# The recurrence's opening: key products stored a second time in the inverses' layout, the first v load on GpSimd, one mask earlier

## The chip, the cores and the metric

The kernel runs on one core of a Trainium2 chip. Five engines work from queues of their own, each in order: TensorE (PE, with its weight loads as PEld), VectorE (DVE), ScalarE (ACT), GpSimd (POOL) and SyncE (SP). Transfers are given out by SP, ACT or GpSimd and carried out by 16 shared DMA engines. The metric is the time on the device in microseconds (us), lower is better.

## The reference

A two-layer hybrid over 256 tokens of width 2048, in float32. Layer 0 is an RWKV7 mixer with 32 heads of 64: four projections `r, k, v, z`, a decay and a gate from low-rank products, and the recurrence. Layer 1 is an attention with three branches (compressed, selected, window), which plays no part here.

```python
mixed = u[None] + xx[None] * mu[:, None, None, :]
rkvz = jnp.einsum('nbtd,nde->nbte', mixed[:4], w_rkvz)
...
def step(S, inp):                       # the recurrence, once per token
    r_t, w_t, k_t, v_t, a_t, b_t = inp
    sa = jnp.einsum('bhvk,bhk->bhv', S, a_t)
    S = S * w_t[:, :, None, :] + sa[..., None] * b_t[:, :, None, :] + v_t[..., None] * k_t[:, :, None, :]
    return S, jnp.einsum('bhvk,bhk->bhv', S, r_t)
```

## The kernel before

**Weights.** Weight matrices stream through PE in pieces. SP loads a piece of 512 KB (`wraw`, L178, five buffers), ACT copies each half into a rounded high part (`whi`, L206), DVE subtracts to get the low part (`wlo`, L191), and PE multiplies three times (high by high, low by high, high by low: L569, L570, L572, or L587, L588, L589 where the weight is the stationary side). These matmuls are the bulk of the kernel. In the recurrence they serve as filling between its small steps: `fill(n)` runs some of them from the projection of `r`.

**The recurrence by chunks.** The 256 tokens are four chunks of 64, and the 32 heads are 16 pairs `j`. Within a chunk, the token-by-token recurrence is turned into matrix products with the inverse of a triangular 64x64 matrix. In the *key phase* (up to about 348 us) `stage_k(j)` forms that matrix's key products `ab` for the pair `j` (L726), copies them to `abs` (L728) and stores 128x256 of them to the scratch tensor `abd` in HBM (L729). `stage_t(b)` inverts the 32x32 diagonal blocks of eight pairs at a time (`b` is 0 or 1), 128 blocks, one in each partition of `invA`; each block row is 32 numbers, 128 bytes. It reads these blocks from `abd` with eight transfers of 16x32x32 (L756); for `b` = 1 two of the eight go to GpSimd, the rest to SP. Then come many small DVE steps (L786 to L806), which the planner places one at a time ("pump"); the results go to `tnd` and `yvd` in HBM.

**The opening.** Two pairs make a unit U, and the recurrence runs through eight units. Unit 0 needs a prologue, and its order on every engine is that of the code (a manual schedule): load `spl` (the pair's scaled keys), `Yb`, `a`; clear `uv`; some filling; then the second inverse begins, and its input is loaded; load `t`; filling; load `Yb` of unit 1; filling; load `spl` of unit 1; and then `load_v(0)` on ACT's queue (four transfers of 64 KB from `vd` into `uv`, L932). After that the list `PROLOGUE` is worked off: `R` scales r (L960 to L963); a number is filling; `G` is a product whose result ACT copies to `gs` (L972, L974); `Y` multiplies by `gs` (L981) and completes the inverse in `Yb`; `B` transposes (L991); `V6` or `V9` are six or nine pumps of the second inverse on DVE; `A` forms attention products (L1005, L1007), `M2` masks one of them into AMA, `M0` and `M1` the other into AMR (L1013). Then the units' phases begin with the *removal* (L1022), which needs AMA and `uv`. After `Y`, `load_a(1)` gives GpSimd the `a` and `t` loads of unit 1.

## Time and profile before

| | |
|---|---|
| three runs | 1164.82, 1166.99, 1160.91 us; median 1164.82 |
| profiled execution | 1160.9 us; its span is 1160.9 us too, so next to nothing lies around it |
| instructions | 25551 |
| DMA packets | 231325, of them 49808 under 512 B |
| bytes moved | 225.26 MB, mean 194 GB/s |

Times are from the span's start. A timeline row has the start, the length, the engine, line and operation, out<-in by the program's names, the number of instructions put together, and in brackets the idle time ahead with what ended it. SPq, ACTq and POOLq are issues of transfers by these engines. In the table of waits stand the engine and line that waited, what for, the sum, the times and the longest. The columns of the stretches are told where one is shown.

### The profile page before, as it was taken

How to read it: one execution, taken by the hardware profiler on the slowest of the kernel's cores; microseconds unless marked ns; L12 is line 12 of the kernel's file. 1: busy time of each engine (PE TensorE's matmuls, PEld its weight loads, DVE VectorE, ACT ScalarE, POOL GpSimd, SP SyncE). 2: the span in 40 equal slices, each digit the busy share in tenths (PEclk: the TensorE clock that was granted, in tenths of full speed). 3: DMA queues.
4: the chain of work that ended last, by engine and by line, in shares of the span. 5: the costliest groups of instructions: out<-in, count | busy, mean ns of one | idle time of the engine just before them, and what ended most of it. 6: DMA issues, size and time to landing. Idle time of an engine off the chain costs nothing.

```text
span 1160.9 us, 25551 instructions
## 1 busy us (share of the span) xinstructions
PE 1121.0 (97%) x9414; PEld 981.0 (85%) x9414; DVE 843.0 (73%) x1876; ACT 715.4 (62%) x1680; POOL 328.1 (28%) x418
## 2 busy tenths in 40 slices
PE   7999999999997999998999999999999999999996
PEld 6878899888987888897788888887989989988886
DVE  6999966679895887566567876764577888785564
ACT  4767777577763456565556766665656666665453
POOL 1300045324346455563000010100333333333011
PEclk8999999999998999999999999999999999999999
DMA  6458877787869768874467758685745353635752
GB/s 230 157 186 245 237 211 247 234 201 209 258 213 245 196 176 254 234 201 128 125 209 247 209 174 275 186 259 161 195 136 152 96 148 106 164 95 185 282 186 105
DMA packets 231325, 225.26 MB, mean 194 GB/s; under 512 B 49808, under 2 KB 179200, under 8 KB 230816
## 3 DMA queue, kind: packets, MB, share of 16 engines
q1 hardware_dynamic: 225280, 218.55, 64.1%
q0 software_dynamic: 4832, 4.82, 1.8%
q8 instruction: 74, 1.21, 0.4%
q14 instruction: 51, 0.42, 0.1%
q10 hardware_dynamic: 1088, 0.26, 0.1%
HBM read 200.48 MB, written 23.10 MB: 193 GB/s over the span
## 4 chain that ended last, share of the span: by engine, by line
PE 81%; DVE 9%; DMA 3%; ACT 3%; issue 3%; SPq 1%; POOL 0%; ACTq 0%; POOLq 0%; DVEq 0%
PE bank L570 13%; PE bank L572 13%; PE bank L569 13%; PE bank L587 8%; PE bank L588 7%; PE bank L589 7%; PE bank L234 5%; DVE wlo L191 3%; PE pair L572 1%; PE pair L569 1%; ACT whi L206 1%; PE pair L570 1%; PE pair L1051 1%; PE bank L726 1%; DMA wraw<-in_b_w_o_dram 1%
## 5 line engine op out<-in xcount | busy, mean ns | idle before, releaser
L191 DVE TENSOR_TENSOR wlo<-wraw,whi 128x512 fp32r<-128x512 f32 (+2 forms) x616 | 437.8, 724 | 157.2 <-ACT whi L206 152.5
L206 ACT ACTIVATE whi<-wraw 128x512 fp32r<-128x512 f32 (+2 forms) x664 | 401.7, 620 | 209.4 <-PE bank L572 92.8
L587 PE MATMUL bank<-mh,whi 128*128 128x256 f32 (+1 forms) x800 | 236.1, 295 | 0.2 <-issue 0.2
L570 PE MATMUL bank<-wlo,mh 128*128 128x512 f32 (+3 forms) x608 | 229.1, 379 | 2.0 <-DVE wlo L191 2.0
L588 PE MATMUL bank<-ml,whi 128*128 128x256 f32 (+1 forms) x800 | 228.3, 285 | 1.1 <-issue 1.1
L589 PE MATMUL bank<-mh,wlo 128*128 128x256 f32 (+1 forms) x800 | 227.8, 285 | 0.0
L572 PE MATMUL bank<-whi,ml 128*128 128x512 f32 (+3 forms) x608 | 227.6, 377 | 0.0
L569 PE MATMUL bank<-whi,mh 128*128 128x512 f32 (+3 forms) x608 | 202.2, 378 | 0.8 <-ACT mh L419 0.8
L587 PEld LDWEIGHTS bank<-mh,whi 128*128 128x128 f32 (+1 forms) x800 | 151.8, 190 | 6.5 <-issue 0.9
L588 PEld LDWEIGHTS bank<-ml,whi 128*128 128x128 f32 (+1 forms) x800 | 152.3, 190 | 3.0 <-issue 1.3
L589 PEld LDWEIGHTS bank<-mh,wlo 128*128 128x128 f32 (+1 forms) x800 | 151.9, 190 | 1.3
L570 PEld LDWEIGHTS bank<-wlo,mh 128*128 128x128 f32 x608 | 114.3, 188 | 20.5 <-DVE wlo L191 3.1
L569 PEld LDWEIGHTS bank<-whi,mh 128*128 128x128 f32 x608 | 113.4, 188 | 19.0 <-ACT mh L419 1.1
L572 PEld LDWEIGHTS bank<-whi,ml 128*128 128x128 f32 x608 | 114.3, 188 | 17.8 <-issue 0.4
L191 POOL TENSOR_TENSOR wlo<-wraw,whi 128x512 fp32r<-128x512 f32 (+2 forms) x48 | 62.5, 1303 | 190.3 <-ACT whi L206 158.5
L570 PE MATMUL bank<-wlo,kvh 128*128 128x512 f32 x192 | 76.9, 401 | 0.0
L572 PE MATMUL bank<-whi,kvl 128*128 128x512 f32 x192 | 76.1, 396 | 0.0
L569 PE MATMUL bank<-whi,kvh 128*128 128x512 f32 x192 | 67.4, 396 | 0.0
L419 ACT ACTIVATE mh<-mtmp 128x256 fp32r<-128x256 f32 x96 | 38.9, 410 | 21.5 <-DVE mtmp L426 20.3
L426 DVE SCALAR_TENSOR_TENSOR mtmp<-xx,prm,xn 128x256 f32<-128x256 f32 x96 | 47.9, 506 | 1.2 <-POOL xx L458 1.0
L570 PEld LDWEIGHTS bank<-wlo,kvh 128*128 128x128 f32 x192 | 36.1, 188 | 8.7 <-issue 0.4
L420 DVE TENSOR_TENSOR ml<-mtmp,mh 128x256 fp32r<-128x256 f32 x96 | 41.6, 441 | 2.0 <-ACT mh L419 1.8
(332 smaller groups left out, 1871.3 us busy)
## 6 DMA issues: line engine op xcount, KB each, us to landing
wraw<-in_a_w_rkvz_dram SPq DMA_DIRECT2D x128, 512.0 KB, 5.2
wraw<-in_kv_w_dram SPq DMA_DIRECT2D x48, 512.0 KB, 4.6
wraw<-in_b_w_in_dram SPq DMA_DIRECT2D x40, 512.0 KB, 4.2
wraw<-in_a_w_o_dram SPq DMA_DIRECT2D x32, 512.0 KB, 4.6
wraw<-in_b_w_o_dram SPq DMA_DIRECT2D x32, 512.0 KB, 4.6
spd<-sp SPq DMA_DIRECT2D x16, 642.0 KB, 4.7
spl<-spd SPq DMA_DIRECT2D x16, 642.0 KB, 6.8
wraw<-in_b_w_in_dram SPq DMA_DIRECT2D x24, 384.0 KB, 3.3
```

The costliest lines, as they stand in the source:

```text
L191: eng.tensor_tensor(lv, src, hv.bitcast(F32), op=OP.subtract)
L206: self.nc.scalar.activation(hv, src, AF.Copy)
L234: return fn(*args, **kw)
L419: S.activation(h, src, AF.Copy)
L420: V.tensor_tensor(l, src, h.bitcast(F32), op=OP.subtract)
L426: V.scalar_tensor_tensor(m, xx[:, k, :], mu[:, k:k + 1], xn[:, k, 1:], op0=OP.mult, op1=OP.add)
L569: PE.matmul(o, mh[:, ts], wh[:, 0, :], start=k == ends[0], stop=False)
L570: PE.matmul(o, mh[:, ts], wl[:, 0, :], start=False, stop=False)
L572: PE.matmul(o, ml[:, ts], wh[:, 0, :], start=False, stop=k == ends[1])
L587: PE.matmul(o, wh[:, s, :], mh, start=k == 0 and first, stop=False, **kw)
L588: PE.matmul(o, wh[:, s, :], ml, start=False, stop=False, **kw)
L589: PE.matmul(o, wl[:, s, :], mh, start=False, stop=k == NK - 1, **kw)
```

## The change

Each pair's key products are stored twice: besides `abd`, four new transfers on SP (32x4x32 each, one for each head and half) write the two kinds of diagonal blocks into `abdd[b]`, which has the layout of `invA`, 1024 numbers for each of the 128 partitions. `stage_t` reads them in one transfer of 128x1024 on SP instead of eight. `load_v(0)` goes to GpSimd and stands behind `load_a(0, "T")`. In `PROLOGUE`, `M2` stands ahead of the second `V9`.

```diff
-PROLOGUE = ("R0", "R1", 6, "G", "B0", 4, "I", "Y", "B1", 2, "V6", "A0", 2, "V9", "A1", "V9", "M2", "M0", "M1", 2)
+PROLOGUE = ("R0", "R1", 6, "G", "B0", 4, "I", "Y", "B1", 2, "V6", "A0", 2, "V9", "A1", "M2", "V9", "M0", "M1", 2)
...
+    abdd = [dram.tile([128, 1024], F32, name=f"abdd{i}") for i in range(2)]
...
         nc.sync.dma_start(abd[j], abs_)
+        for h in range(2):
+            for q in range(2):
+                r0 = 64 * h + 32 * q
+                dst = bass.AP(tensor=abdd[j // 8].tensor, offset=abdd[j // 8].offset + (q * 16 + (j % 8) * 2 + h) * 1024,
+                              ap=[[32, 32], [32 * 1024, NCH], [1, 32]])
+                nc.sync.dma_start(dst, abs_[r0:r0 + 32, :].rearrange("p (c s) -> p c s", c=NCH)[:, :, 32 * q:32 * q + 32])
...
-        for c in range(NCH):
-            for q in range(2):
-                u0 = (c * 2 + q) * 16
-                src = bass.AP(tensor=abd.tensor, offset=abd.offset + 8 * b * 128 * T + q * 32 * T + c * 64 + q * 32,
-                              ap=[[64 * T, 16], [T, 32], [1, 32]])
-                (G if b and c == 3 else nc.sync).dma_start(A[u0:u0 + 16], src)
+        nc.sync.dma_start(A.rearrange("p a b -> p (a b)"), abdd[b])
...
     load_a(0, "T")
+    load_v(0, G)
     fill(10)
...
     fill(8)
-    load_v(0, nc.scalar)
```

PE's order does not change. In the rows below, brackets hold the semaphores that an instruction waits for: an engine's name, or a lane (DMAHW0 to 7 of SP and ACT, DMASW0 to 7 of GpSimd), on which the transfer that had the lane before must have landed.

SP at the end of the key phase and in the opening, before:

```order
L729 DMA abd<-abs 128x256 [waits Activation_49]
L923 DMA spl_4524<-spd 128x1284 [waits DMAHW2_49,PE_49]
...
L178 DMA wraw<-in_a_w_rkvz_dram 128x8x128 [waits DMAHW0_49,DVE_49]
L756 DMA invA<-abd 16x32x32 [waits DMAHW1_49]
L756 DMA invA<-abd 16x32x32 [waits DMAHW2_49]
L756 DMA invA<-abd 16x32x32 [waits DMAHW3_49]
L756 DMA invA<-abd 16x32x32 [waits DMAHW4_49]
L756 DMA invA<-abd 16x32x32 [waits DMAHW5_49]
L756 DMA invA<-abd 16x32x32 [waits DMAHW6_49]
L178 DMA wraw<-in_a_w_rkvz_dram 128x8x128 [waits DMAHW7_49,DVE_49]
```

and after:

```order
L730 DMA abd<-abs 128x256 [waits DMAHW6_49,Activation_49]
L736 DMA abdd_1612<-abs 32x4x32 [waits DMAHW7_49]
L736 DMA abdd_1612<-abs 32x4x32 [waits DMAHW0_49]
L736 DMA abdd_1612<-abs 32x4x32 [waits DMAHW1_49]
L736 DMA abdd_1612<-abs 32x4x32 [waits DMAHW2_49]
L925 DMA spl_4583<-spd 128x1284 [waits DMAHW3_49,PE_49]
...
L178 DMA wraw<-in_a_w_rkvz_dram 128x8x128 [waits DMAHW1_49,DVE_49]
L758 DMA invA<-abdd_1612 128x1024 [waits DMAHW2_49]
L178 DMA wraw<-in_a_w_rkvz_dram 128x8x128 [waits DMAHW3_49,DVE_49]
```

Four stores stand behind `abd`, the weight load waits for the lane of the third of them, and one issue stands where six were. Between the rows shown are, in both, the second `spl` and four `Yb`.

ACT ahead of `gs`, before:

```order
L206 ACTIVATE whi<-wraw 128x512 [waits DMAHW0_49,DVE_49,PE_49]
L932 DMA uv_4672<-vd 64x4x64 [waits DMAHW3_49]
L932 DMA uv_4672<-vd 64x4x64 [waits DMAHW5_49]
L932 DMA uv_4672<-vd 64x4x64 [waits DMAHW6_49]
L932 DMA uv_4672<-vd 64x4x64 [waits DMAHW7_49]
L206 ACTIVATE whi<-wraw 128x512 [waits DVE_49,PE_49]
L206 ACTIVATE whi<-wraw 128x512 [waits DMAHW0_49,DVE_49,PE_49]
L974 ACTIVATE gs<-pair_4913 128x256 [waits PE_49]
```

and after:

```order
L206 ACTIVATE whi<-wraw 128x512 [waits DMAHW5_49,DVE_49,PE_49]
L206 ACTIVATE whi<-wraw 128x512 [waits DVE_49,PE_49]
L206 ACTIVATE whi<-wraw 128x512 [waits DMAHW1_49,DVE_49,PE_49]
L976 ACTIVATE gs<-pair_4965 128x256 [waits PE_49]
L994 ACTIVATE bkt_4741<-pair_4927 128x384 [waits PE_49]
```

The four `uv` loads are gone from between the splits. DVE around the mask AMA, after:

```order
L795 TENSOR_TENSOR invX<-invT,invM 128x64 [waits DVE_49]
L797 TENSOR_TENSOR invM_4796<-invM_4796,invX 128x64 [waits DVE_49]
L1015 TENSOR_TENSOR ama_4733<-bank_4727,cst 128x512 [waits PE_49]
L795 TENSOR_TENSOR invX<-invT,invM 128x64 [waits DVE_49]
L797 TENSOR_TENSOR invM_4796<-invM_4796,invX 128x64 [waits DVE_49]
L799 COPY invT<-invM_4796 128x4x4x4 [waits DVE_49]
L805 TENSOR_TENSOR invX<-invA,invM_4796 128x128 [waits Activation_49]
```

Before, eleven more steps of the inverse, the four rows below it and seven like them, stood ahead of that mask; AMR keeps its place behind them. GpSimd, from its clearing of `uv` to the `Yb` loads of unit 1, after:

```order
L929 MEMSET uv_4731 64x8x64 [waits Pool_49]
L854 DMA t_4587<-tnd_1613 32x4x32 [waits DMASW2_49]
...
L934 DMA uv_4731<-vd 64x4x64 [waits DMASW6_49]
L934 DMA uv_4731<-vd 64x4x64 [waits DMASW7_49]
L934 DMA uv_4731<-vd 64x4x64 [waits DMASW0_49]
L934 DMA uv_4731<-vd 64x4x64 [waits DMASW1_49]
L1170 MEMSET ones_4746 128x2 [waits DMAHW3_49,PE_49,Pool_49]
L1171 MEMSET Yb_4730 128x512
L862 DMA Yb_4730<-yvd_1615 32x4x32 [waits DMASW2_49,Pool_49]
```

Two `invA` pieces, which stood between the clearing and the four `t` loads, are gone, and four `uv` loads stand behind `t`.

## The prediction

> **What bounds the kernel now.** I read the page first: the busy times, then the chain that ended last.

> ```profile
> PE 1121.0 (97%) x9414; PEld 981.0 (85%) x9414; DVE 843.0 (73%) x1876; ACT 715.4 (62%) x1680; POOL 328.1 (28%) x418
> PE 81%; DVE 9%; DMA 3%; ACT 3%; issue 3%; SPq 1%; POOL 0%; ACTq 0%; POOLq 0%; DVEq 0%
> ```

> TensorE (PE) is busy 97% of the span and carries 81% of the chain. So a change pays only where PE stands idle or runs at a lower clock, about 40 us of the 1160.9, and what it adds elsewhere costs only if PE waits for it. The table of stretches says where that is around the change: the key phase ahead of the recurrence, and then the opening.

> ```profile
> 300.00:348.00 48.00, 47.80 (x337) 41.53 (x336) 42.05 (x77) 33.78 (x78) 23.28 (x26) 1.00 0.76 237
> 348.00:385.00 37.00, 27.86 (x371) 26.36 (x369) 22.37 (x65) 12.38 (x27) 23.22 (x44) 0.86 1.11 252
> ```

> The columns are the length, the busy time of PE, PEld, DVE, ACT and POOL, PE's granted clock, the DMA share and GB/s. The key phase keeps PE busy 47.80 of 48 us. The opening leaves it idle 9.1 of 37 us, at a mean clock of 0.86, while the DMA engines are full (1.11). Next the waits between 345 and 385 us (sum, times, longest):

> ```profile
> PE pair L981 <- ACT gs L974: 7.0, 1, 7.0
> PE pair L1022 <- issue: 2.1, 1, 2.1
> ```

> Two waits of PE make all of it: 7.0 us before Y (L981) and 2.1 us before the removal (L1022). PE's timeline gives their places:

> ```profile
> 364.39 0.28 PE L589 MATMUL bank<-mh,wlo 128*128 128x256 f32 x1
> 371.71 1.08 PE L981 MATMUL pair<-gs,t 64*64 64x32 f32 x32 [7.04 <-ACT gs L974]
> 382.33 0.54 PE L1022 MATMUL pair<-uv,ama 128*64 128x64 f32 x8 [2.10 <-issue]
> 389.57 0.71 PE L972 MATMUL pair<-Yb,a 64*64 64x32 f32 x32
> ```

> and cutting the stretch finer gives the price of the clock:

> ```profile
> 364.70:371.70 7.00, 0.00 (x0) 0.02 (x1) 0.85 (x2) 1.51 (x4) 5.56 (x11) 0.71 0.97 221
> 371.70:378.00 6.30, 6.29 (x95) 5.89 (x95) 5.41 (x23) 2.57 (x6) 4.51 (x8) 0.51 1.10 312
> 378.00:382.30 4.30, 2.23 (x56) 1.82 (x56) 3.55 (x15) 0.52 (x2) 2.26 (x4) 1.00 1.21 252
> ```

> During the 7-us wait the clock falls, and the 6.3 us behind it run at 0.51. At full clock that work is 6.3 x 0.51 = 3.2 us, so the long wait costs another 3.1 us. Behind the 2.10-us wait the clock stays 1.00. The opening thus loses 7.0 + 3.1 + 2.1 = 12.2 us.

> Who holds gs (L974)? It has nothing but ACT's queue in front of it:

> ```profile
> 357.04 0.63 ACT L206 ACTIVATE whi<-wraw 128x512 fp32r<-128x512 f32 x1 [0.81 <-PE bank L588]
> 366.50 3.60 ACTq L932 DMA_DIRECT2D uv<-vd  x4
> 370.19 1.15 ACT L206 ACTIVATE whi<-wraw 128x512 fp32r<-128x512 f32 x2 [12.52 <-DMA wraw<-in_a_w_rkvz_dram]
> 371.25 0.36 ACT L974 ACTIVATE gs<-pair 128x256 f32<-128x256 f32 x1
> ```

> The row at 370.19 names a weight transfer, but that one was issued at 355.36 (SP's timeline, next) and had 14 us. What stood in the way are the four loads of v, which ACT issues only at 366.50, each waiting for its turn behind earlier transfers of SP:

> ```profile
> 348.66 1.73 SPq L729 DMA_DIRECT2D abd<-abs  x1
> 352.25 1.93 SPq L860 DMA_DIRECT2D Yb<-yvd  x4
> 355.36 0.40 SPq L178 DMA_DIRECT2D wraw<-in_a_w_rkvz_dram  x1
> 356.18 8.22 SPq L756 DMA_DIRECT2D invA<-abd  x6
> 364.50 2.10 SPq L178 DMA_DIRECT2D wraw<-in_a_w_rkvz_dram  x2
> ```

> SP needs 8.22 us for the six input pieces of the second inverse. So the chain is: slow issues on SP, then the v loads on ACT, then two splits, then gs, then Y.

> **The change, part by part.** *The v loads leave ACT.* Their 3.60 us and the wait ahead of them vanish from ACT. gs then stands behind the two splits (1.15 us), the second of which needs the weight piece issued now at 355.36. SP has four more stores ahead of it.

> ```profile
> abd<-abs SPq DMA_DIRECT2D x16, 128.0 KB, 4.9
> vd<-vst SPq DMA_DIRECT2D x16, 128.0 KB, 3.8
> uv<-vd SPq DMA_DIRECT2D x28, 64.0 KB, 4.8
> uv<-vd ACTq DMA_DIRECT2D x4, 64.0 KB, 8.8
> invA<-abd SPq DMA_DIRECT2D x14, 64.0 KB, 4.3
> wraw<-in_a_w_rkvz_dram SPq DMA_DIRECT2D x128, 512.0 KB, 5.2
> ```

> (times, KB each, median us from issue to landing.) No store of 128-byte runs is in the trace. A store's issue is bounded by a Yb issue (1.93 / 4 = 0.48 us) and the slow abd issue (1.73 us). I take 0.55, next to the Yb row, since those four are the same 32x4x32 pattern in the other direction: 4 x 0.55 = 2.2 us, which puts the weight issue at 357.6. It also waits for one of these stores to land; issued at 351.5 and with the 4.9 us of abd that is 356.4, so no more. Landing is 357.6 + 5.2 = 362.8, the splits end at 364.2 (1.15 us and the handover), gs at 364.6, and Y starts at 365.0, when PE has just run dry (364.39 + 0.28). Bounds: 364.7, and 369.7 if each store takes 1.73 us (4 x 1.18 = 4.7 us later). The long wait shrinks from 7.04 us to about 0.3, and with it goes the half clock: 3.1 us.

> The trace kept the clock through 2.10 us idle and lost it in 7.04. [...]

> *One inverse input instead of eight.* The eight pieces, 128-byte runs, 4096 packets, become one transfer with 4-KB runs. SP gives it out near 358.2, one issue of 0.4 us in place of 8.22. The nearest landing is 5.2 us (wraw, as many bytes): 363.4. On the far side stands spl (642 KB), given out behind abd (from 350.4) and waited for until 360.12, 9.7 us: 367.9.

> ```profile
> 360.12 0.43 DVE L960 TENSOR_TENSOR spl<-bank,spl 128x256 f32<-128x256 f32 x1 [1.50 <-DMA spl<-spd]
> ```

> spl too goes out 2.2 us later, so this work of DVE and the low half of the split behind it, which PE takes up about 1.2 us before it runs dry, move from 360.8 to 363.0; that is just in time for Y at 365.0, and I book nothing.

> *M2 ahead of the second V9.* DVE's rows of before, where AMA is the tensor that the removal waits for:

> ```profile
> 370.85 1.29 DVE L191 TENSOR_TENSOR wlo<-wraw,whi 128x512 fp32r<-128x512 f32 x2 [9.38 <-ACT whi L206]
> 373.62 0.18 DVE L767 COPY invT<-invA 128x16 f32<-128x16 f32 x1 [0.22 <-DMA spl<-spd]
> 378.13 0.22 DVE L795 TENSOR_TENSOR invM<-invM,invX 128x64 f32<-128x64 f32 x1
> 381.55 0.68 DVE L1013 TENSOR_TENSOR ama<-bank,cst 128x512 f32<-128x512 f32 x1
> ```

> By the order after, AMA follows the step at 378.13, so it starts 4.7 us behind the inverse's first copy (373.62 to 378.35) instead of 7.9. That copy follows DVE's halves of the splits and two clears. It came 2.3 us behind the end of the splits on ACT (370.19 + 1.15 = 371.3, against 373.62); from their end at 364.2 I get 366.5, still behind the landing at 363.4. AMA runs from 371.2 to 371.9, and the removal starts at 372.0. PE's own work between Y and the removal is 3.2 + 2.2 = 5.4 us at full clock, so it is dry from 370.5 and waits 1.5 us. With 367.9 for the landing the removal is at 373.4. The gain of the opening is 382.33 - 372.0 = 10.3 us; the losses agree: 6.7 of the long wait, 3.1 of clock, 0.6 of the short one are 10.4.

> *What comes late next.* GpSimd's queue now carries the four v loads, and behind them are the eight Yb loads of unit 1, two scalings and the a and t loads of unit 1, which G and Y of unit 1 wait for.

> ```profile
> 356.71 1.26 POOL L756 DMA_DIRECT2D invA<-abd  x2 [4.03 <-issue]
> 357.96 2.19 POOL L852 DMA_DIRECT2D t<-tnd  x4
> 364.57 3.26 POOL L860 DMA_DIRECT2D Yb<-yvd  x6 [2.42 <-DMA invA<-abd]
> 369.73 0.57 POOL L849 DMA_DIRECT2D a<-abd  x1
> t<-tnd POOLq DMA_DIRECT2D x32, 16.0 KB, 4.6
> ```

> Two input pieces of the inverse leave this queue, with their 1.26 us and the 4.03 us that they waited for SP. So t goes out from 352.7 and v from 354.9, to 357.5 with 2.19 us and some room. The last Yb load waits for the last v load to land: 357.5 plus 4.8 (SP's row) to 8.8 (ACT's, in the crowded stretch), 362.3 to 366.3. I take 364. Then come one more issue (0.55) and the scalings with 1.9 (from 364.57 + 3.26 to 369.73 before), so a starts at 366.5; the eight issues need 8 x 0.57 = 4.6 us, and t's last lands near 366.5 + 4.6 + 4.6 = 375.7, at worst 378. G of unit 1 is due at 389.57 - 10.3 = 379.3, its Y 1.3 us later. It is covered by 1.3 to 3.8 us; if the cover is gone, what is over is lost one for one. I take 0.3 us.

> *Stores in the key phase.* 16 times four stores of 16 KB. PE stays busy if SP's weight loads are not late, and SP mostly waits for its consumers there (165 to 348 us):

> ```profile
> SPq L178 <- DVE wlo L191: 38.5, 20, 4.0
> ```

> Ahead of weight loads alone that is 38.5 us of free time of SP. 64 stores at 0.48 to 1.73 us are 31 to 111 us, at my 0.55 they are 35. The DMA engines: the crowded stretch at 362 to 366 us moved

> ```profile
> DMA packets 2268, 0.36 MB, mean 90 GB/s; under 512 B 2194, under 2 KB 2265, under 8 KB 2267
> ```

> in 4 us, 1.8 ns a packet with all sixteen engines full. 512 packets per head pair are 0.9 us, sixteen of them 14 us in 183, 8% more on a share of 0.76. I book 0.5 us, with 0 to 2 as bounds; it can't gain. The landing of the first inverse's input falls beside filled PE and counts nothing.

> Sum: 10.3 - 0.3 - 0.5 = 9.5 us. The profiled execution has 1160.9 us and is the fastest of the three runs; the median, 1164.8, is 3.9 above it. Against the profile I get 1151.4, against the median 1155.3; I say 1155.

> **The rivals.** *A, the wait only shortens.* If a store takes 1.73 us, or if it lands late and the weight piece behind it waits, Y starts at 369.7, a wait of 5.0 us. If this drops the clock, 5.4 us of work need 8.5 and the removal is at 378.2: gain 4.1, less 0.8, 3.3, hence 1161.5 against the median, within 0.5%. For it: the slow abd issue stands at this very place, and the engines are full. Against it: the Yb issues right behind it took 0.48. [...]

> *B, GpSimd's queue becomes the bound.* If v needs more than 8.8 us there, or a start waits for lanes, G of unit 1 waits 2 to 4 us: 1158. For it, v, Yb, a and t then stand in one queue; against it, 1.3 us of cover even at the ACT row's 8.8.

> *C, slower.* The stores hold up the weights throughout the key phase. At 1.73 us each they need 111 us of SP, far more than those 38.5 us; where a weight load comes 1 us late per head pair, 16 us are lost: 1171. Above 0.6 us per pair the gain is gone, above 1 us it is slower by 0.5%. Against it, only the last abd issue is slow in this trace.

> *D, it does not do what it says*: gs is held by the weight piece alone, as the row at 370.19 names it. Then Y stays at 371.7 and M2 alone gives 2.1 us: 1163. The 14 us since that piece's issue speak against it.

> **How the numbers follow.** The forecast 0.65, A 0.13, B 0.10, C 0.06, D 0.06. A measurement of this kernel tells some 0.5% (5.8 us) from no change. The forecast's own range is 1151 (10.3 and no give-back, on a run at the profile's level) to 1158. For 8 in 10, I add B and A and reach to 1162; the low end is 1149, if the short wait goes too. Faster by over 0.5% is below 1159: nearly all of the forecast, most of B and the milder third of A, 0.74; same, the rest of A and B, D, 0.20; slower, 0.06.

> **What would show it.** Y within 1.5 us after PE runs dry, and no clock under 1.00 behind it; the removal 7 us behind Y; one invA of 4-KB runs landing ahead of 367; no longer v rows on ACT; G of unit 1 without a wait; PE in 300 to 348 us still at 47.5 or more. The prediction is wrong if PE waits over 2 us at Y or at G of unit 1, or if waits for wraw turn up in the key phase.

## The result, and the profile after

The kernel after takes 1154.39 us (median of 4 runs, 1152.51 to 1156.80), the one before 1165.90 beside it: a ratio of 0.9914, interval 0.9895 to 0.9932. Timed a second time, beside two of the experiments, it took 1152.49 us, 0.9901 (0.9882 to 0.9921). 1155 had been forecast. The ratios and their 95% intervals are the ones on record; a gain in us below is worked out from the ratio, and the quotient of two medians differs from it by up to 0.0015 (1.7 us). The profiled execution has a span of 1153.6 us, 7.3 less than that of before; a second profile of the same kernel has 1150.4, 10.5 less.

The two stretches that were shown of before:

```profile
300.00:348.00 48.00, 47.88 (x340) 41.98 (x341) 42.23 (x78) 32.67 (x76) 24.84 (x29) 1.00 0.77 235
348.00:385.00 37.00, 32.17 (x529) 30.02 (x529) 27.23 (x82) 17.09 (x40) 24.29 (x45) 1.00 1.10 294
```

In the same 37 us PE is busy 32.2 us instead of 27.9, and now all of it at full clock: 1.00 instead of 0.86. The key phase, with its added stores, is as full as before. The waits of PE between 345 and 385 us:

```profile
PE pair L1024 <- issue: 2.0, 1, 2.0
PE bank L993 <- DVE mb L963: 1.6, 1, 1.6
PE pair L983 <- issue: 0.7, 1, 0.7
```

and their places on PE's timeline (the lines have moved by one or two: L983 is Y, L1024 the removal, L993 the transposes, here the first of unit 1):

```profile
363.77 0.33 PE L983 MATMUL pair<-gs,t 64*64 64x32 f32 x9 [0.69 <-issue]
371.68 0.42 PE L1024 MATMUL pair<-uv,ama 128*64 128x64 f32 x5 [1.99 <-issue]
378.54 0.44 PE L993 MATMUL bank<-cst,spl 128*128 128x128 f32 x2 [1.64 <-DVE mb L963]
```

The 7.04 us before Y have become 0.69. The wait for the mask at the removal is still there with 2 us. A wait that before did not have, 1.64 us for DVE's scaling of unit 1, has come up. SP, GpSimd and DVE at the opening:

```profile
347.28 2.02 SPq L730 DMA_DIRECT2D abd<-abs  x1
349.36 1.90 SPq L736 DMA_DIRECT2D abdd<-abs  x4
355.43 0.46 SPq L178 DMA_DIRECT2D wraw<-in_a_w_rkvz_dram  x1
355.94 0.59 SPq L758 DMA_DIRECT2D invA<-abdd  x1
```

```profile
354.10 2.44 POOL L934 DMA_DIRECT2D uv<-vd  x4
364.14 0.55 POOL L862 DMA_DIRECT2D Yb<-yvd  x1 [1.57 <-DMA uv<-vd]
367.04 0.57 POOL L851 DMA_DIRECT2D a<-abd  x1
371.08 0.55 POOL L854 DMA_DIRECT2D t<-tnd  x1 [0.23 <-issue]
```

```profile
365.27 0.49 DVE L769 COPY invT<-invA 128x16 f32<-128x16 f32 x1
370.90 0.68 DVE L1015 TENSOR_TENSOR ama<-bank,cst 128x512 f32<-128x512 f32 x1
378.07 0.41 DVE L963 TENSOR_TENSOR mb<-bank,spl 128x256 f32<-128x256 f32 x1
```

The four stores took SP 1.90 us, the eight input pieces have become one issue of 0.59, and GpSimd's queue has its last t load out at 371.6. DVE's row for unit 1's scaling was this in the kernel before:

```profile
385.56 0.41 DVE L961 TENSOR_TENSOR mb<-bank,spl 128x256 f32<-128x256 f32 x1
```

The inverse's copy moved up by 8.35 us (373.62 to 365.27), the mask by 10.65, the scaling by 7.49. PE's removal came 10.65 us earlier, and PE then met DVE at the scaling.

PE's order is the same in before, after and most of the experiments but for a few neighbours that change places, so times between the same two of its instructions can be compared. (In stores_twice and stores_wide some filling between 254 and 312 us moved too.) This table is worked out from PE's timelines; E is the end of the last matmul ahead of Y (364.39 + 0.28 in before), R the removal, B unit 1's first transposes (387.39 in before), F a filling matmul (L588) at 417.21 in before. "First inverse" runs from a filling matmul at 244.93 in before to the first key product of the tenth pair (L726, 263.35).

| kernel | ratio to before | first inverse | from there to E | wait at Y | Y to R | R to B | B to F | E to F |
|---|---|---|---|---|---|---|---|---|
| before | 1 | 18.42 | 101.31 | 7.05 | 10.62 | 5.06 | 29.82 | 52.54 |
| after | 0.9914 | 17.17 | 101.50 | 0.69 | 7.91 | 6.86 | 29.45 | 44.90 |
| after, second profile | 0.9901 | 16.04 | 101.64 | 0.02 | 8.11 | 6.86 | 29.57 | 44.57 |
| v_only | 0.9980 | 18.87 | 101.29 | 0 | 13.29 | 7.36 | 29.15 | 49.73 |
| inv_only | 0.9954 | 15.87 | 101.49 | 4.09 | 10.24 | 8.03 | 28.75 | 51.11 |
| m2_only | 0.9983 | 18.48 | 101.28 | 7.69 | 7.85 | 7.00 | 29.89 | 52.44 |
| m2_back | 0.9939 | 15.76 | 101.52 | 0.87 | 10.68 | 7.64 | 28.71 | 47.91 |
| second_only | 0.9927 | 17.96 | 101.51 | 0.21 | 8.96 | 6.65 | 29.52 | 45.34 |
| stores_twice | 1.0024 | 23.35 | 103.35 | 1.09 | 6.96 | 6.88 | 29.45 | 44.39 |
| stores_wide | 1.0033 | 23.11 | 103.00 | 2.03 | 6.88 | 6.90 | 29.90 | 45.71 |

From F to the end the profiles of these kernels differ by up to 3.3 us (743.25 to 746.51), though the work there is the same. After's first profile is 1.95 us longer there than before, its second 1.05; of the first, 1.5 us lie ahead of 480 us, where PE waits 2.0 us at L1040 (L1038 in before) instead of 0.7. The cause was not traced.

### The profile page after: what moved, and what is told of

Read it like the earlier page. It is cut to its first block, busy times and chain, and to the rows that moved or that the text cites. A ratio compares the mean times of both kernels' runs of the same rounds, so it can differ in the third digit from the quotient of the medians.

```text
span 1153.6 us, 25609 instructions
## 1 busy us (share of the span) xinstructions
PE 1119.0 (97%) x9414; PEld 979.6 (85%) x9414; DVE 844.8 (73%) x1876; ACT 715.8 (62%) x1680; POOL 328.3 (28%) x420
## 3 DMA queue, kind: packets, MB, share of 16 engines
q8 instruction: 74, 1.21, 0.4%
## 4 chain that ended last, share of the span: by engine, by line
PE 79%; DVE 11%; issue 3%; ACT 3%; DMA 3%; POOL 0%; SPq 0%; ACTq 0%; POOLq 0%; DVEq 0%
PE bank L570 13%; PE bank L569 13%; PE bank L572 13%; PE bank L587 7%; PE bank L589 7%; PE bank L588 7%; PE bank L234 5%; DVE wlo L191 3%; PE pair L572 1%; PE pair L569 1%; PE pair L570 1%; DVE invX L805 1%; ACT whi L206 1%; PE pair L1053 1%; DVE mtmp L426 1%
## 5 line engine op out<-in xcount | busy, mean ns | idle before, releaser
L191 DVE TENSOR_TENSOR wlo<-wraw,whi 128x512 fp32r<-128x512 f32 (+2 forms) x616 | 438.6, 725 | 149.9 <-ACT whi L206 145.2
L206 ACT ACTIVATE whi<-wraw 128x512 fp32r<-128x512 f32 (+2 forms) x664 | 402.0, 619 | 205.6 <-PE bank L572 94.5
L588 PE MATMUL bank<-ml,whi 128*128 128x256 f32 (+1 forms) x800 | 227.7, 285 | 0.0
L589 PE MATMUL bank<-mh,wlo 128*128 128x256 f32 (+1 forms) x800 | 227.3, 285 | 0.0
L588 PEld LDWEIGHTS bank<-ml,whi 128*128 128x128 f32 (+1 forms) x800 | 151.7, 190 | 1.8
L589 PEld LDWEIGHTS bank<-mh,wlo 128*128 128x128 f32 (+1 forms) x800 | 151.4, 189 | 1.3
L191 POOL TENSOR_TENSOR wlo<-wraw,whi 128x512 fp32r<-128x512 f32 (+2 forms) x48 | 62.4, 1301 | 190.4 <-ACT whi L206 158.6
## 6 DMA issues: line engine op xcount, KB each, us to landing
wraw<-in_a_w_rkvz_dram SPq DMA_DIRECT2D x128, 512.0 KB, 5.5
wraw<-in_kv_w_dram SPq DMA_DIRECT2D x48, 512.0 KB, 4.4
wraw<-in_b_w_in_dram SPq DMA_DIRECT2D x40, 512.0 KB, 4.2
wraw<-in_a_w_o_dram SPq DMA_DIRECT2D x32, 512.0 KB, 4.6
wraw<-in_b_w_o_dram SPq DMA_DIRECT2D x32, 512.0 KB, 4.3
```

Source lines behind the costliest of these rows:

```text
L191: eng.tensor_tensor(lv, src, hv.bitcast(F32), op=OP.subtract)
L206: self.nc.scalar.activation(hv, src, AF.Copy)
L588: PE.matmul(o, wh[:, s, :], ml, start=False, stop=False, **kw)
L589: PE.matmul(o, wl[:, s, :], mh, start=False, stop=k == NK - 1, **kw)
```

## Experiments

The theory at the start: DVE's queue sets the opening's end, so a part is worth what it brings DVE's work forward (theory 1). The rival is the sum on record, in which each wait of PE taken away counts by itself (theory 2).

### Each part alone

v_only is the kernel before with one move:

```diff
     load_a(0, "T")
+    load_v(0, G)
...
-    load_v(0, nc.scalar)
```

> Before, with only load_v(0) moved to GpSimd (the inverse's input still in eight pieces, M2 still behind both V9). Theory 1 (the opening is set by DVE's queue: its work from the second inverse's first copy to unit 1's scaling; what a part is worth is how much earlier that copy starts): PE no longer waits 7 us at Y, but the copy now waits for the last invA piece, issued at 364.5 and landing near 369; it starts 4.5 us earlier than in the kernel before (373.6), the removal waits 5 us or more, and the whole gains 4 to 5 us. Theory 2 (the recorded sum: ACT's queue held PE, and each wait of PE taken away is a gain of its own): Y at 365, clock kept, 7.0 + 3.1 us gained, some 10.

Measured: 1160.73 us, ratio 0.9980 (0.9966 to 0.9994). PE's waits from 360 to 385 us:

```profile
PE pair L1022 <- issue: 6.4, 1, 6.4
PE pair L981 <- DMA t<-tnd: 0.4, 1, 0.4
```

The 7-us wait at Y is gone, as both theories said, so ACT's queue did hold PE. But a wait of 6.4 us stands at the removal in its place, where 2.1 was. Theory 2 is wrong here (2.3 us gained, interval 0.7 to 4.0, not 10). Theory 1 had this wait (5 us or more), and DVE's timeline shows it: the inverse's first copy still waits for transfers, behind SP's six pieces, and the mask behind it comes at 376.76:

```profile
367.62 0.18 DVE L767 COPY invT<-invA 128x16 f32<-128x16 f32 x1 [3.56 <-DMA uv<-vd]
```

(The row names a v load, which came last by the profile; the copy itself reads `invA`.) But theory 1's gain of 4 to 5 us is too high. What it left out is in the stretches of the removal's wait and behind it (length; busy PE, PEld, DVE, ACT, POOL; clock, DMA share, GB/s):

```profile
371.20:377.50 6.30, 0.00 (x0) 0.00 (x0) 5.46 (x18) 0.51 (x2) 5.60 (x12) 0.64 1.07 316
377.60:382.90 5.30, 5.30 (x62) 4.83 (x63) 4.45 (x14) 1.51 (x5) 3.71 (x6) 0.50 1.24 223
```

The clock fell again: 5.3 us at 0.50, which by the same reckoning as the prediction's cost half of them.

inv_only is after with the v loads back on ACT and M2 back behind both V9, so that the new stores and the single input transfer are left:

```diff
-    load_v(0, G)
...
+    load_v(0, nc.scalar)
...
-"A1", "M2", "V9", "M0"
+"A1", "V9", "M2", "M0"
```

> After, but load_v(0) back on ACT behind the filling, and M2 behind both V9: only the extra stores and the single invA transfer are left of the change. The v loads on ACT then wait for lanes of transfers that land at 362 to 364. Theory 1: gs some 2 to 3 us later than after, Y near 366 with 2 to 3 us of wait and no loss of clock, the inverse's first copy 2 to 3 us later than after, gain over before 5 to 6 us. Theory 2: it lacks M2's share as well, 3 us, gain over before 2 to 4 us. If the v loads on ACT were the cause whatever stands on SP, Y still waits 5 us or more and the gain is under 2 us.

Measured: 1157.45 us, ratio 0.9954 (0.9938 to 0.9971), 5.3 us, where theory 1 had 5 to 6; the interval, 3.4 to 7.2 us, reaches into theory 2's 2 to 4 as well. Y waits 4.1 us, more than theory 1 had, and the clock fell for 3.4 us behind it, which theory 1 had ruled out. By the table only 1.4 us of it come from the opening (52.54 to 51.11); 2.6 come from the first inverse, where none were expected. On ACT's timeline the four v loads still take 6.60 us and hold the splits and gs:

```profile
356.70 6.60 ACTq L934 DMA_DIRECT2D uv<-vd  x4
363.41 1.15 ACT L206 ACTIVATE whi<-wraw 128x512 fp32r<-128x512 f32 x2 [9.56 <-DMA uv<-vd]
```

m2_only is the kernel before with the list's new order alone:

```diff
-"A1", "V9", "M2", "M0"
+"A1", "M2", "V9", "M0"
```

> Before, with only M2 moved ahead of the second V9. Theory 2 (and the recorded rival in which only M2 counts): the 2.10 us wait at the removal goes, 2.1 us gained. Theory 1: the removal starts 2.1 us earlier, but unit 1's transposes (L991) then wait for DVE's scaling (L961, which ended 1.4 us before PE came to them), so 0.5 to 1.5 us are left; Y's 7-us wait and the half clock are as before.

Measured: 1161.97 us, ratio 0.9983 (0.9971 to 0.9994). PE's waits from 370 us on show theory 1's new wait, and the profile's opening has gained 0.1 us; the runs' 2.0 us (interval 0.7 to 3.4) don't tell the theories apart.

```profile
PE pair L981 <- issue: 7.7, 1, 7.7
PE bank L991 <- DVE mb L961: 1.4, 1, 1.4
```

In the opening (E to F) the parts alone bring 2.8, 1.4 and 0.1 us, together 4.3. All three bring 7.6. Each part alone leaves one wait of more than 4 us somewhere, and the half clock behind it.

### What the mask is worth when the rest is in

m2_back is after with that order changed back:

```diff
-"A1", "M2", "V9", "M0"
+"A1", "V9", "M2", "M0"
```

> After, with M2 behind both V9 again. Both theories: AMA is 3 to 3.5 us later and the removal of unit 0 waits 5 us instead of 2.0. Theory 1: DVE's queue carries the same work, so unit 1's scaling comes no later, PE's 1.6 us wait for it (L993) goes, and at Y of unit 1 no more than 1.5 us are left of the 3; the time is within 1.5 us of after. Theory 2: 3 us slower than after.

Measured: 1156.47 us, ratio 0.9939 (0.9926 to 0.9952), 2.9 us above after by the ratios; its interval overlaps a little with after's first and not with the second. The opening is 3.0 us longer, so theory 1 fails: it had no more than 1.5. Theory 2 had 3, but it had failed in v_only; neither theory holds throughout. The wait for the scaling is gone, as theory 1 said, but the removal's wait is long again, and the clock pays:

```profile
PE pair L1024 <- issue: 4.8, 1, 4.8
```

```profile
367.70:372.30 4.60, 0.00 (x0) 0.00 (x0) 3.81 (x16) 0.51 (x2) 2.89 (x5) 0.95 1.15 266
372.40:378.40 6.00, 6.00 (x65) 5.53 (x66) 5.01 (x14) 1.97 (x5) 2.60 (x6) 0.50 1.13 299
```

After has no such stretch: from 371.7 to 378.5 its clock is 1.00. The mask alone moved an idle time; with the other parts it cut the last wait down to 2 us. m2_back_split, made from m2_back, tries the clock by itself:

```diff
-"R1", 6, "G", "B0", 4, "I"
+"R1", 2, "G", "B0", 2, "I"
...
-"M0", "M1", 2)
+"M0", "M1", 8)
```

> M2 behind both V9 as in m2_back, but six units of filling are moved from ahead of Y (6 and 4 become 2 and 2) to behind AMR (2 becomes 8); the work is the same. Clock theory: m2_back loses less by its 4.8-us wait at the removal than by the half clock behind it (removal to unit 1's transposes 7.6 us instead of 5.1). If the moved filling splits the idle time so that no wait is over 3 us, the clock stays at 1.00, removal to transposes take 5 to 6 us, and the opening is 2 us shorter than in m2_back. If the wait at the removal stays over 4 us, the clock falls again and the time is that of m2_back. Theory without the clock (only the idle time counts): the same idle time, the same time as m2_back, whatever the split.

Measured: 1156.80 us, ratio 0.9935 (0.9915 to 0.9956), the time of m2_back. The wait was split into 2.2 and 2.1 us, and yet the clock fell, though for 3.4 us instead of 6.8:

```profile
362.10:365.51 3.41, 1.21 (x26) 0.94 (x26) 1.83 (x5) 0.49 (x1) 2.63 (x7) 1.00 1.20 261
365.51:368.92 3.41, 3.41 (x49) 3.29 (x42) 3.03 (x16) 0.00 (x0) 3.17 (x7) 0.50 1.04 349
```

PE was busy for 1.21 of the 3.41 us ahead of the fall. So the expectation's 3 us for a single wait, an estimate of the author's that lies between the 2.10 us behind which before kept its clock and the 4.8 us behind which m2_back lost it, doesn't hold, and the experiment doesn't confirm the clock's share; it is inconclusive for the total. What does hold is in the last section.

### The first inverse

second_only is after, but for pairs 0 to 7 without the extra stores, and with the old eight input pieces for the first inverse.

```diff
-        for h in range(2):
+        for h in range(2 if j >= 8 else 0):
...
-        nc.sync.dma_start(A.rearrange("p a b -> p (a b)"), abdd[b])
+        if b:
+            nc.sync.dma_start(A.rearrange("p a b -> p (a b)"), abdd[b])
+        else:
+            ...  # the eight pieces from abd
```

> After, but only the second inverse (b = 1) reads the new layout: for the first eight pairs the extra stores are left out, and the first inverse's input comes in eight pieces from abd on SP again. Theory A (the first inverse's eight slow issues on SP held back the second half of the key phase): PE's stretch around the first inverse (about 245 to 263 us) takes 18.4 us as in the kernel before, 1.2 to 2.7 us more than with the new layout; the opening as after. Theory B (these 1 to 3 us are chance of the single profiled executions, or come from elsewhere): that stretch takes 15.8 to 17.2 us. Total by A 1.2 to 2.7 us above after, by B the same.

Measured: 1155.91 us, ratio 0.9927 (0.9906 to 0.9947). The total can't tell the 1 to 3 us, but the stretch can. With the old input it takes 17.96 to 18.87 us in four kernels. With the new one it takes 17.17 and 16.04 in after's two profiles, 15.87 in inv_only and 15.76 in m2_back, and 15.6 to 15.8 in the four other kernels that have it and no further stores. On ACT's queue, first of before and then of after's second profile, the inverse's copy (L817, L819) stands in front of the work of the next pair:

```profile
250.21 0.54 ACT L817 ACTIVATE invM<-invT 128x64 f32<-128x64 f32 x2 [1.81 <-DVE invT L797]
251.43 0.46 ACT L678 ACTIVATE t<-bank,prm 128x256 f32<-128x256 f32 x1
```

```profile
246.61 0.54 ACT L819 ACTIVATE invM<-invT 128x64 f32<-128x64 f32 x2 [1.83 <-DVE invT L799]
247.84 0.47 ACT L679 ACTIVATE t<-bank,prm 128x256 f32<-128x256 f32 x1
```

and PE waits there for that t (1.1 us) and for a norm of the same queue, 2.3 us in before with one wait for GpSimd, and 0.4 in after's second profile:

```profile
PE bank L681 <- ACT t L678: 1.1, 1, 1.1
PE bank L699 <- ACT rnx L696: 0.9, 2, 0.5
```

```profile
PE bank L700 <- ACT rnx L697: 0.4, 1, 0.4
```

So theory A holds in its effect: an earlier first inverse is worth 1.2 to 2.7 us here. Its words blamed SP's issues; the traces name the inverse's chain through DVE and ACT, which starts later when the eight pieces land later.

### What the stores cost

stores_twice writes each of the 64 extra stores a second time, to a tensor that nothing reads.

```diff
-                nc.sync.dma_start(dst, abs_...)
+                for d in (abdd, abd2):
+                    ...
+                    nc.sync.dma_start(dst, abs_...)
```

> After, with each of the 64 extra stores issued a second time to a tensor that nothing reads. Measures what the stores cost: PE's stretch behind the first inverse (eight pairs, L726 to the opening) takes 101.5 us with the stores and 101.3 without; if that is their price, 101.7 with twice as many, and the opening 1.5 to 2.5 us later at its weight piece (four more issues on SP). [...]

Measured: 1166.96 us, ratio 1.0024 (1.0009 to 1.0040). That is 14.5 us above after, timed beside it: more than the change gains. The first four stores of a pair cost 0.2 us over the last seven pairs by the table (101.31 against 101.50); four more cost 1.9 there (103.35), 7.3 at the first inverse (23.35 against 16.04 in after's second profile) and 3.9 in the stretch ahead of it (from 183 us in before to the first inverse, 61.8 to 65.7 us). On SP, stores wait for the landing of weights that had their lanes before (SP's waits from 165 to 360 us, with what its weight loads still wait for DVE; then PE's):

```profile
SPq L738 <- DMA wraw<-in_a_w_rkvz_dram: 15.1, 17, 1.4
SPq L178 <- DVE wlo L191: 9.7, 11, 2.9
```

```profile
PE bank L701 <- ACT rnx L698: 6.5, 4, 4.5
```

The 38.5 us that SP's weight loads waited for DVE in before were 25.4 in after's second profile and have shrunk to 9.7. The 7.3 us at the first inverse are one chain. SP gives out its input at 243.75, 10.6 us later than in after's second profile (PE itself is 4.3 us later there), and the inverse's first copy stands in DVE's queue ahead of `cum` (L695), which ACT's queue needs:

```profile
249.89 0.18 DVE L771 COPY invT<-invA 128x16 f32<-128x16 f32 x1 [7.78 <-DMA invA<-abdd]
252.64 0.42 ACT L704 ACTIVATE sp<-cum 128x256 f32<-128x256 f32 x1 [7.15 <-DVE cum L695]
```

So PE waits 4.5 us for `rnx`, a few rows on in ACT's queue, and the clock stands at 0.50 from 253.04 to 259.87 with 6.15 us of work in it, another 3.1. The last kernel asks whether the cost lies in the queue or in the small runs:

```diff
+                nc.sync.dma_start(wide[j, r0:r0 + 32, :], abs_[r0:r0 + 32, 0:128])
```

> As stores_twice, at the same places on SP and with as many bytes, but the second set writes 32 rows of 512 bytes per store (32 packets) to a tensor that nothing reads, instead of 128 runs of 128 bytes. It tells apart why twice the stores cost 13 to 14 us. If it is SP's queue (0.43 to 0.5 us for each issue, and eight lanes, in which the next weight loads stand behind the stores), the time is that of stores_twice within 4 us. If it is the small runs on the DMA engines (512 packets more per pair), most of it goes, and the time is within 4 us of after.

Measured: 1168.50 us, ratio 1.0033 (1.0015 to 1.0051), the same as stores_twice, with 32 packets of 512 bytes in place of 128 of 128. Landing times of the two kinds, side by side in this kernel:

```profile
abdd<-abs SPq DMA_DIRECT2D x64, 16.0 KB, 3.2
wide<-abs SPq DMA_DIRECT2D x64, 16.0 KB, 2.7
```

So it is the four more transfers on SP, not the size of their runs; both kernels store the same bytes. The stores with runs of 128 bytes land 0.5 us later here, but in stores_twice, where both sets have runs of 128 bytes, the first set lands later as well (3.6 against 3.0 us). How much of the 14 us is issue time and how much lanes was not separated.

### Trying for more

masks_first starts from the view that the waits left are DVE's.

```diff
-"V6", "A0", 2, "V9", "A1", "M2", "V9", "M0", "M1", 2)
+"V6", "A0", 2, "A1", "M2", "M0", "M1", "V9", 2)
```

> After, with all three masks ahead of every V9, and one of the two V9 left out (its nine pumps come later by themselves): the list ends A1, M2, M0, M1, V9, 2. DVE theory (after's remaining waits are DVE's: 2.0 us for AMA at the removal, 1.6 us for unit 1's scaling, both behind pumps of the second inverse): both go, and the opening is 2.5 to 3.5 us shorter; up to 1.5 us come back where the inverse must be done, ahead of unit 4's loads near 436 to 443 us. Net 1 to 3 us faster than after. Rival: the pumps' later places hold up the units' own DVE work by as much, and the time is that of after.

Measured: 1162.54 us, ratio 0.9991 (0.9973 to 1.0010), 9 us worse than after. The masks came early and PE didn't wait for them. But one row of ACT's timeline shows what the pumps had to be early for:

```profile
374.66 0.51 ACT L819 ACTIVATE invM<-invT 128x64 f32<-128x64 f32 x2 [7.88 <-DVE invT L799]
```

The inverse's copies stand in ACT's order ahead of X of unit 0. While ACT waited 7.88 us for DVE's pumps, PE waited 3.8 us for X (L1042), the clock fell for another 3.4 us, and near 445 us, where the inverse must be done, PE waited 4.0 us for X a second time:

```profile
PE pair L1047 <- ACT X L1042: 3.8, 1, 3.8
PE pair L1047 <- ACT X L1042: 4.0, 1, 4.0
```

masks_clear is the same with the clearing of invT moved ahead:

```diff
-        if not b:
-            V.memset(Tm, 0.0)
+        V.memset(Tm, 0.0)
         if b:
             yield lambda: "inv" in phase_done
-            V.memset(Tm, 0.0)
```

> masks_first, and the 0.9-us clearing of invT for the second inverse moved ahead of the wait for its start, into DVE's idle time before 363 us. DVE theory: the first copy of the second inverse and all behind it come 1 us earlier than in masks_first where DVE is what PE waits for; with the masks early little of it is left, 0 to 1 us faster than masks_first. Rival: no difference.

Measured: 1161.40 us, ratio 0.9977 (0.9963 to 0.9992); against masks_first the intervals overlap, so the move of the clearing by itself is not decided.

scale_clear has that clearing, after's list, and the scaling of unit 1's first pair one phase earlier:

```diff
+            if U == 0 and v == 0:
+                scale_r(1, 0)
             sch.pump()
...
-            if v == 1 and U + 1 < NU:
+            if v == 1 and 0 < U and U + 1 < NU:
```

> After, with two moves on DVE that leave its work the same: the 0.9-us clearing of invT for the second inverse goes ahead of the wait for its start, and the scaling of unit 1's first pair moves from behind to ahead of the pumps that follow unit 0's removal. DVE theory: PE's 1.6 us wait for that scaling (L993) goes, the 2.0 us wait for AMA shrinks by up to 0.9, as far as the inverse's input has landed; the opening is 1.5 to 2.5 us shorter than after, total 1 to 2.5 us faster. Rival (as in masks_first, something else is queued behind: ACT's copies of the inverse, GpSimd's scaling): no gain.

> The kernel after once more, unchanged, beside the next two and with a second profile: 0.990 to 0.993 of before. If the clock's drops depend on where a wait falls and not on its length alone, the second profile may show one in the opening (1.5 to 3 us), which the first didn't; PE's stretch around the first inverse 15.6 to 17.2 us.

Measured: scale_clear 1154.90 us, ratio 0.9912 (0.9890 to 0.9935); after 1152.49, 0.9901 (0.9882 to 0.9921). The wait at L993 is gone and the removal's is 0.7 us, as expected, but a wait of 1.9 us for DVE's statistics (L1075) comes up two steps on, and then the clock falls for 6.8 us:

```profile
378.77:382.19 3.42, 1.47 (x57) 1.33 (x58) 3.27 (x13) 2.05 (x7) 0.65 (x2) 1.00 1.06 294
382.19:389.02 6.83, 6.83 (x82) 6.09 (x85) 2.84 (x13) 2.88 (x8) 0.00 (x0) 0.50 0.61 201
```

PE was busy 1.47 of the 3.42 us ahead. The gain of 1 to 2.5 us that the DVE theory had did not come. After's second profile has no fall of the clock in the opening. No version beat after.

## Why the prediction was right

The time was right, 1155 against 1154.4, and so was the mechanism of the longest wait: four v loads on ACT, behind SP's slow issues, held gs and Y. v_only shows that by itself. The sum came out partly by luck, since two of its terms were wrong in opposite directions. The key phase ended 1.6 us earlier than in before (E at 363.08 instead of 364.67, in the second profile at 361.06), which was not forecast, so a time from the span's start that fits is not yet a fit. Point by point, with after's first and second profile against the profile of before:

- *The long wait and the clock.* 7.05 us became 0.69 and 0.02; 0.3 had been said. Y to the removal, 10.62 us, took 7.91 and 8.11; from 372.0 minus 365.0 it was to be 7.0. The clock stayed at 1.00. But "the trace kept the clock through 2.10 us idle" is half of what that trace has: near 552 us, past the stretches that the prediction shows, the clock of before fell behind a wait of 1.99 us. The clock at the removal could have gone either way (last section).
- *The weight piece* was to be issued at 357.6 and split near 363; it was issued at 355.43 and its split began at 362.77. Two errors cancelled: SP was 2.2 us ahead of the forecast (1.1 because the `abd` issue ended earlier, 0.3 because the stores took 0.48 us each instead of 0.55, 0.8 in the issues between), and the landing took up to 7.3 us instead of 5.2.
- *The mask.* AMA ran from 370.90, 371.2 had been said; but from E it is 7.8 us instead of 6.5, since the mask came 5.6 us behind the inverse's first copy (370.90 less 365.27) and not 4.7. The wait left at the removal is 2.0 and 1.1 us, against 1.5; the second profile has another of 1.0 us ahead of it (L1007).
- *GpSimd's queue* went as worked out: v issued up to 356.5 (357.5 said), the last Yb at 364.14 (364), a from 367.04 (366.5). G of unit 1 didn't wait for it, so rival B fell. (The larger cover, 379.3 less 375.7, is 3.6 us and not 3.8.)
- *What comes late next* is the term that was mis-sized, and on the wrong engine. 0.3 us had been booked for G of unit 1; removal to F took 36.3 and 36.4 us instead of 34.9, 1.4 and 1.5 us given back. DVE holds PE at unit 1's scaling, 1.64 us. DVE's scaling had moved up by 7.5 us, and PE's removal ahead of it by 10.65; the argument followed every queue but DVE's past the mask.
- *The key phase.* "The landing of the first inverse's input falls beside filled PE and counts nothing" was the step that failed: that input brought 1.2 and 2.4 us. The stores' cost of 0.5 was nearly right: the one place where they show, the last seven pairs, is 0.2 to 0.3 us longer.
- *The sum.* In the opening 7.6 and 8.0 us instead of 10.0 (1.2 and 0.8 of it lost up to the removal, the rest behind it), at the first inverse 1.2 and 2.4 instead of 0: two errors of opposite sign, 8.9 and 10.4 less 0.2 to 0.3 for the stores, against 9.5.
- *Rival C* was given 6 in 100, on the ground that only one issue was slow and that SP has 38.5 us free. That was enough for these four stores, of 0.48 us each; four more cost 14 us. The price of a loss had been worked out per late weight, but not how near the edge was.
- *Rival A* fell: neither the issues of the four stores (1.90 us) nor their landing held the weight piece up so far that Y waited more than 0.69 us.
- *Rival D* is out: with the v loads moved and all else left, Y doesn't wait for the weight piece.

## What to carry to other kernels

When the engine that sets the time waits, the time to be gained is not the wait but the wait up to the next thing it will meet, with the clock on top: three parts that brought 2.8, 1.4 and 0.1 us alone brought 7.6 together, since with each part alone one long wait was left, and with it the half clock. Follow every engine's queue past the change, also that of the engine whose work is only reordered: here it was DVE's. And an in-order queue with free time has an edge: four more small transfers per step cost 0.2 us over seven steps, the next four cost 14 in the kernel, half of it because one transfer was given out later and DVE's queue stood still for it. So measure the added thing twice over before trusting its cover.

## What the runs showed of the hardware

The clock's fall is not a matter of one wait's length. In the 14 profiles, waits of 3.8 us and more, from 100 us on, were always followed by a stretch at 0.50 (in before, v_only, m2_only, inv_only, m2_back, both kernels with more stores and both with the masks first). Shorter ones were sometimes: second_only, with waits of 0.2 and 1.5 us ahead, fell, in nearly the opening where after, with 0.7 and 2.0, did not. Divided at the edges of the falls, in second_only, then in after, which has no edge here and is divided by steps from its own fall at 541.39, then in before near 552 us:

```profile
364.42:367.83 3.41, 1.90 (x54) 1.56 (x53) 3.27 (x12) 0.52 (x2) 3.06 (x7) 1.00 1.15 274
367.83:371.24 3.41, 3.41 (x56) 3.07 (x56) 2.65 (x12) 0.63 (x1) 3.22 (x6) 0.50 1.04 370
```

```profile
367.30:370.72 3.42, 2.40 (x58) 1.99 (x56) 3.04 (x16) 0.63 (x1) 3.42 (x7) 1.00 1.03 378
370.72:374.13 3.41, 2.45 (x57) 2.26 (x57) 2.76 (x11) 1.31 (x4) 1.67 (x4) 1.00 1.16 267
```

```profile
548.60:552.01 3.41, 1.20 (x41) 1.08 (x41) 3.27 (x12) 1.17 (x4) 1.25 (x1) 1.00 0.31 84
552.01:555.42 3.41, 3.41 (x8) 2.35 (x8) 2.34 (x5) 0.32 (x1) 0.42 (x1) 0.50 0.31 88
```

What share of idle time was enough in these runs can be read off that grid. The 14 profiles have 4210 of its steps, here called windows, at full clock between 100 and 1140 us. With PE's busy time as the profile models it, the clock fell behind all 28 in which PE was busy less than half, and behind none in which it was busy 0.57 or more; of the four between, two fell (0.53 and 0.56) and two did not (0.51 and 0.54). In second_only a window with PE busy 1.90 of 3.41 us was enough. After's wait of 2.0 us at the removal lay across two windows, with PE busy 2.40 of 3.42 and 2.45 of 3.41 us, and the clock stayed. Wholly inside one window it would have left at most 1.4 of 3.41 us, less than half. Of the 1.99 us in before, 1.2 lay in the window from 548.60, with smaller gaps beside them; PE was busy 1.20 of 3.41 us, and the clock fell. In after's two profiles the grid starts 2.1 and 3.3 us behind the span's start (541.39 and 539.22 us, less 158 and 157 windows), so the same wait of one kernel can fall into one window or across two. That part of a short wait's cost is chance is worked out from this; no run moved a wait against the grid on purpose.
